# A hybrid decoder trunk on one core: TensorE's order where attention, output projection, norms and MLP meet

## The chip, the core and the metric

The kernel runs on one core of a Trainium2 chip. The core has a matrix engine (TensorE, PE in the profile's rows), whose weight loads are listed apart (PEld), a vector engine (VectorE, DVE), a scalar engine (ScalarE, ACT), GpSimd (POOL) and SyncE (SP), which only issues transfers here. Each engine works through its own list of instructions in order; semaphores make it wait for the others. The metric is the device time of one execution in microseconds (us).

## What is computed

A decoder trunk of two layers on 256 tokens of width 1024, in float32. Cut to what matters here, a layer is

```
h = rms_norm(x, ln1_gain[l]);  proj = h @ w_in[l]            # 1024 -> 2866 columns
o_nsa, o_mla, o_ret = three attention groups on slices of proj
x = x + concatenate([o_nsa, o_mla, o_ret]) @ w_out[l]         # 1024 -> 1024
h = rms_norm(x, ln2_gain[l])
x = x + square(relu(h @ w_up[l])) @ w_down[l]                 # 1024 -> 4096 -> 1024
```

and a last rms_norm follows the second layer. The change lies at the two places of a layer where x is normalised: between `w_out` and `w_up`, and between `w_down` and the next layer's `w_in`.

## The kernel before

**Tiles.** The 256 tokens are two tiles of 128 partitions, t = 0 and 1. `xs` holds the residual x of both tiles. Nearly every operand of a matmul is split into two parts, `hi` (a cast by ScalarE, line 140) and `lo` (the rest, a subtraction by VectorE, line 141); `mm3` (lines 146 to 148) makes a product of three matmuls, lo·hi, hi·lo and hi·hi. The up projection (`up_half`, lines 1023 and 1024) needs two instructions per product, a wide one of 512 columns and a narrow one of 256.

**Weights.** They come in units through one stream `W`: a load by SyncE into one of five raw buffers, then a split into one of five hi and lo buffers. A unit is split up to four units ahead of its use, unless `W.hold(key)` stops the splitting ahead of unit `key`; `W.release(after, n)` lets it go on, with the new splits issued behind the two instructions `after`. A unit's raw buffer takes the next load once its split is done.

**Norms.** The factor of a row is applied behind the projection, so ahead of it only the gain is needed. `norm_half(t, h, gain, eng)` takes half h (512 columns) of tile t: a product `xg` of xs and the gain (line 504), four transposes of 128x128 into a bank `ps_xT` (line 506), and the split of that bank into the two parts of `xT`, by ScalarE and VectorE. `sum_sq` is ScalarE's sum of squares (`junk`, line 512).

**The order.** Each engine's list is fixed before the run: a scheduler simulates the engines and takes at each point the ready instruction of highest priority (`prio`, from a table), and `tc.issue_after(x)` makes it place what stands inside behind x.

**From attention to MLP.** The second token tile's work comes last in some places and first in others: `TORD = (1, 0)`, so tile 1 goes first here. I call it the first tile, and tile 0 the second. The values of the selected and sliding attention (`nsa_values`) transpose probabilities into `ps_pT`, copy them to `pT` (`g == 0` by ScalarE, line 868, the other by VectorE, line 870), multiply them with the values into `l_oT`, and split that into `mixT`. The output projection runs over eight slices `kt` of mixT in the order 3, 4, 6, 7, 5, 0, 1, 2; only the last three need `nsa_values`. Its four banks `l_po` are two for the first tile (numbers 1823 and 1824 for halves 0 and 1 in the orders below) and two for the second (1821 and 1822). Then, at lines 999 to 1004, for the first tile and then the second, half by half, VectorE adds `l_po` to xs (line 1002) and `norm_half` is called, with GpSimd for the first tile's products and VectorE for the second's. Splits were held ahead of the unit `(l, "wu", 1, 0)` and are released behind the last of the four splits of xT; the four sums of squares come behind it too.

**MLP.** The up projection has 16 chunks c of 256 columns, each in two halves i of its depth. The first two chunks start together, half 0 of both and then half 1 of both (lines 1055 to 1057), into four banks `ps_up`. For each chunk ScalarE copies a part of `ps_up` to `u_s` and VectorE adds the rest (lines 1034 and 1035), which frees the bank; chunk 2 takes the banks of chunk 0. The down projection gathers in four banks `l_pd`.

**To the next layer.** For tile 0 and then tile 1, half by half, VectorE adds `l_pd` to xs and `norm_half` follows; the splits held ahead of the fourth A unit are released behind it, and so are the squares. The first projection of the next layer is chunk A (`inproj`, 434 columns, four weight units of two k slices each); within a unit it runs tile 0 and then tile 1. ScalarE evacuates the result to `l_a` (line 570, scaled by `l_rstd`), and TensorE transposes it (`ps_cT`, line 599).

Of the kernel before, what the change touches and what calls it, by code (L numbers as in the profile page):

```python
# [77 lines left out]
def tile_hybrid_trunk(  # L78
# [65 lines left out]
    def mm3(o, a, b, start, stop):  # L144

        nc.tensor.matmul(o, a[1], b[0], start=start, stop=False)  # L146
        nc.tensor.matmul(o, a[0], b[1], start=False, stop=False)  # L147
        nc.tensor.matmul(o, a[0], b[0], start=False, stop=stop)  # L148
# [338 lines left out]
    def norm_half(t, h, gain, eng=nc.vector):  # L487
        sl = slice(h * 512, (h + 1) * 512)
        xg = scr("xg", [P, 512])
        ps = wk("ps_xT", "MN"[h])  # L490
# [14 lines left out]
        for j in range(4):  # L505
            nc.tensor.transpose(ps[:, j * P:(j + 1) * P], xg[:, j * P:(j + 1) * P], ident)
        dst = (slice(None), slice(4 * h, 4 * h + 4), slice(t * P, (t + 1) * P))
        return split(xT[0][dst], xT[1][dst], ps.rearrange("p (k c) -> p k c", k=4))

# [18 lines left out]
    for l in range(DEPTH):  # L528
# [17 lines left out]
        for t in range(2):  # L546
            mean_sq(ms1, ss1, t)
            rsqrt(rstd[:, t:t + 1], ms1[:, t:t + 1])
            nc.gpsimd.tensor_scalar(hrstd[:, t:t + 1], rstd[:, t:t + 1], 0.5, None, op0=ALU.mult)

        if l == 0:
            rope_tables()
        mixT = [p1.tile([P, 8, S], F32R, name=f"{L}mixT{i}", tag=f"mixT{i}") for i in range(2)]

        def inproj(name, evac):
            n = CHUNKS[name][1]
            ps = [acc(f"{L}{name}{t}") for t in range(2)]
            for i, ks in enumerate(KSETS[n]):
                w = W.get((l, name, i))
                for t in range(2):  # L560
                    tk = slice(t * P, (t + 1) * P)
                    for j, kt in enumerate(ks):
                        mm3(ps[t][:, 0:n], (xT[0][:, kt, tk], xT[1][:, kt, tk]),
                            [z[:, j * n:(j + 1) * n] for z in w], start=kt == 0, stop=kt == 7)
# [275 lines left out]
        def nsa_values(t, prs):  # L840
# [38 lines left out]
            for r in range(3):  # L879
                nc.tensor.matmul(oT[:, r * P:(r + 1) * P], vcb[:, r].rearrange("p g d -> p (g d)"), pcT,  # L880
                                 start=False, stop=r == 2)
            split_mix(mixT, 0, 3, t, oT[:, 0:384].rearrange("p (k c) -> p k c", k=3))

        Pcs = [None, None]
# [102 lines left out]
        def outproj(kts, t):  # L987
            for h in range(2):
                for kt in kts:
                    w = W.get((l, "wo", kt))  # L990
                    mm3(po[t][h], [m[:, kt, t * P:(t + 1) * P] for m in mixT],
                        [z[:, h * 512:(h + 1) * 512] for z in w], start=kt == KORDER[0], stop=kt == KORDER[-1])

        W.hold((l, "wu", 1, 0))
        for kts in ((3,), (4,), (6,), (7,), (5,), (0, 1, 2)):
            for t in TORD:
                with prio("po" if len(kts) == 1 else "pol"):
                    outproj(kts, t)
        for t in TORD:
            for h in range(2):  # L1000
                sl = slice(h * 512, (h + 1) * 512)
                nc.vector.tensor_tensor(xs[:, t, sl], xs[:, t, sl], po[t][h], op=ALU.add)
                with prio("norm"):
                    last = norm_half(t, h, gains[f"b{l}"], nc.gpsimd if t == TORD[0] else nc.vector)
        W.release(last, SPLIT_AHEAD)
        with tc.issue_after(last[0].ins):
            for t in TORD:
                for h in range(2):
                    sum_sq(t, h, ss2)
                mean_sq(ms2, ss2, t)  # L1010
                nc.vector.reciprocal(rs2[:, t:t + 1], ms2[:, t:t + 1])


        pd = [[(att(f"{L}pd{t}{h}", "MN"[h]) if t else acc(f"{L}pd{t}{h}")) for h in range(2)] for t in range(2)]
        def up_half(c, i, ps):
# [3 lines left out]
            for k in range(4):  # L1019
                x2 = xT2[:, 4 * i + k].rearrange("p z c -> p (z c)")  # L1020
                for j in range(2):
                    o = k * 256 + j * P
                    nc.tensor.matmul(ps[j], w[0][:, o:o + P], x2, start=i == 0 and k == 0, stop=False)  # L1023
# [153 lines left out]
```

## Time and profile before

| | us |
|---|---|
| median of 3 runs | 675.86 (675.41 to 676.44) |
| profiled execution | 675.34 |
| its span, first to last instruction | 673.5 |
| TensorE busy in the span | 651.4 |
| VectorE busy | 452.4 |
| ScalarE busy | 379.3 |

The granted clock of TensorE was 0.993 of full speed on average over the span. TensorE is busy for 97% of it. The rows that the prediction reads stand further below: a row of a timeline gives the start, the duration, the engine, line, operation, its result and sources, and in square brackets how long the engine had been idle and whose signal ended that.

### The profile page before, as it was taken

Reading aid. Unit: us, or ns where it says so; the run is one execution under the profiler, and the core shown is the slowest. Engines: PE = TensorE matmul, PEld = TensorE weight load, DVE = VectorE, ACT = ScalarE, POOL = GpSimd, SP = SyncE. Lnnn points to the kernel's source line nnn. Section 1 sums busy time; section 2 is a strip of 40 time slices with the busy share of each in tenths; the row PEclk is TensorE's granted clock in tenths of the full one; section 3 lists DMA queues with packets and bytes.
Section 4 is the critical chain, followed back from the end, with each engine's and each line's share of the span. In section 5 each row is a group of like instructions: output and inputs, shape, how many; then the busy total and the mean of one; then the engine's idle time right before and its main releaser. Section 6 shows DMA issues by size and latency. Waiting matters only on the chain.

```text
span 673.5 us, 10414 instructions
## 1 busy us (share of the span) xinstructions
PE 651.4 (97%) x3639; PEld 551.9 (82%) x3639; DVE 452.4 (67%) x1051; ACT 379.3 (56%) x887; POOL 68.0 (10%) x116
## 2 busy tenths in 40 slices
PE   7988999999999999999999999999999999999995
PEld 6987978676788888888889998876688888888884
DVE  6755967677756666666685597677686666666664
ACT  5857776364645454545466786637284454545442
POOL 3510401201000000000023132111100000000000
PEclk7999999999999999999999999999999999999999
DMA  7898544122865656565648574331275656565511
GB/s 232 261 186 257 168 126 123 44 94 68 269 204 165 218 169 215 167 215 167 175 139 200 168 240 133 93 95 34 92 254 181 220 169 208 172 203 181 195 62 62
DMA packets 79508, 111.58 MB, mean 166 GB/s; under 512 B 9432, under 2 KB 67680, under 8 KB 79328
## 3 DMA queue, kind: packets, MB, share of 16 engines
q1 hardware_dynamic: 79424, 110.92, 53.9%
q8 instruction: 28, 0.46, 0.3%
q14 instruction: 24, 0.20, 0.1%
q0 software_dynamic: 32, 0.00, 0.0%
HBM read 109.86 MB, written 1.05 MB: 165 GB/s over the span
## 4 chain that ended last, share of the span: by engine, by line
PE 87%; DMA 5%; DVE 4%; ACT 1%; issue 1%; SPq 1%; POOL 0%; POOLq 0%; ACTq 0%; DVEq 0%
PE ps_up L1023 17%; PE l_pd L146 9%; PE l_pd L147 9%; PE l_pd L148 8%; PE ps_up L1024 8%; PE l_po L146 2%; PE l_po L148 2%; PE l_po L147 2%; PE l_oT L856 2%; DMA raw_B<-in_w_in_dram 2%; PE l_B L146 1%; PE l_B L147 1%; PE l_B L148 1%; PE ps_pT L864 1%; PE ps_s L146 1%; DMA raw_wu<-in_w_up_dram 1%
## 5 line engine op out<-in xcount | busy, mean ns | idle before, releaser
L1023 PE MATMUL ps_up<-xT,hi_wu 128*128 128x512 f32 x512 | 180.0, 394 | 1.3 <-DVE u_s L1035 1.3
L1024 PE MATMUL ps_up<-xT,lo_wu 128*128 128x256 f32 x512 | 140.7, 279 | 0.0
L1023 PEld LDWEIGHTS ps_up<-xT,hi_wu 128*128 128x128 f32 x512 | 95.7, 187 | 24.0 <-DVE u_s L1035 1.7
L141 DVE TENSOR_TENSOR lo_wd<-raw_wd,hi_wd 128x1024 fp32r<-128x1024 f32 x64 | 78.2, 1225 | 52.5 <-ACT hi_wd L140 52.2
L147 PE MATMUL l_pd<-lo_wd,u_h 128*128 128x512 f32 x256 | 100.1, 391 | 0.0
L146 PE MATMUL l_pd<-hi_wd,u_l 128*128 128x512 f32 x256 | 100.1, 391 | 0.0
L148 PE MATMUL l_pd<-hi_wd,u_h 128*128 128x512 f32 x256 | 99.6, 389 | 0.0
L1024 PEld LDWEIGHTS ps_up<-xT,lo_wu 128*128 128x128 f32 x512 | 96.0, 188 | 1.7
L140 ACT CAST hi_wu<-raw_wu 128x512 fp32r<-128x512 f32 x128 | 72.5, 617 | 38.9 <-issue 28.1
L141 DVE TENSOR_TENSOR lo_wu<-raw_wu,hi_wu 128x512 fp32r<-128x512 f32 x128 | 82.2, 687 | 16.6 <-ACT hi_wu L140 16.4
L140 ACT CAST hi_wd<-raw_wd 128x1024 fp32r<-128x1024 f32 x64 | 67.0, 1049 | 32.1 <-PE l_pd L148 21.4
L146 PEld LDWEIGHTS l_pd<-hi_wd,u_l 128*128 128x128 f32 x256 | 48.0, 188 | 10.8
L148 PEld LDWEIGHTS l_pd<-hi_wd,u_h 128*128 128x128 f32 x256 | 48.1, 188 | 10.4
L147 PEld LDWEIGHTS l_pd<-lo_wd,u_h 128*128 128x128 f32 x256 | 48.1, 188 | 8.9
L140 ACT CAST u_h<-u_u 128x512 fp32r<-128x512 f32 x32 | 19.8, 620 | 55.4 <-DVE u_u L1037 55.4
L141 DVE TENSOR_TENSOR lo_B<-raw_B,hi_B 128x192 fp32r<-128x192 f32 (+1 forms) x80 | 28.7, 415 | 23.9 <-ACT hi_B L140 23.8
L1034 ACT COPY u_s<-ps_up 128x256 f32<-128x256 f32 x64 | 23.3, 368 | 36.1 <-PE ps_up L1024 36.1
L1035 DVE TENSOR_TENSOR u_s<-ps_up,u_s 128x256 f32<-128x256 f32 x64 | 26.7, 421 | 24.8 <-ACT u_s L1034 24.8
L140 ACT CAST hi_B<-raw_B 128x192 fp32r<-128x192 f32 (+1 forms) x80 | 25.1, 381 | 18.6 <-DMA raw_B<-in_w_in_dram 13.7
L146 PE MATMUL l_B<-hi_B,xT 128*128 128x384 f32 x96 | 32.9, 351 | 2.3 <-ACT q_sb L570 2.3
L141 DVE TENSOR_TENSOR u_l<-u_u,u_h 128x512 fp32r<-128x512 f32 x32 | 22.1, 691 | 17.8 <-ACT u_h L140 17.8
L148 PE MATMUL l_B<-hi_B,xT 128*128 128x384 f32 x96 | 32.4, 338 | 0.0
(321 smaller groups left out, 1246.5 us busy)
## 6 DMA issues: line engine op xcount, KB each, us to landing
raw_wu<-in_w_up_dram SPq DMA_DIRECT2D x64, 512.0 KB, 4.6
raw_wd<-in_w_down_dram SPq DMA_DIRECT2D x64, 512.0 KB, 4.2
raw_B<-in_w_in_dram SPq DMA_DIRECT2D x24, 384.0 KB, 3.6
raw_wo<-in_w_out_dram SPq DMA_DIRECT2D x10, 512.0 KB, 3.6
raw_A<-in_w_in_dram SPq DMA_DIRECT2D x8, 434.0 KB, 5.0
raw_wo<-in_w_out_dram SPq DMA_DIRECT2D x12, 256.0 KB, 3.8
raw_w<-in_cmp_w_k_dram SPq DMA_DIRECT2D x8, 256.0 KB, 6.3
raw_w<-in_cmp_w_v_dram SPq DMA_DIRECT2D x8, 256.0 KB, 5.8
```

What stands on the lines that cost most here:

```text
L140: a = nc.scalar.copy(out=hi, in_=src)
L141: b = eng.tensor_tensor(lo, src, hi.bitcast(F32), op=ALU.subtract)
L146: nc.tensor.matmul(o, a[1], b[0], start=start, stop=False)
L147: nc.tensor.matmul(o, a[0], b[1], start=False, stop=False)
L148: nc.tensor.matmul(o, a[0], b[0], start=False, stop=stop)
L856: nc.tensor.matmul(oT[gp, 0:384], kv_sb[kt][:, vi, gp], pTs[g][:, 0:384], start=i == 0, stop=False)
L864: last = nc.tensor.transpose(ps[:, r * P:(r + 1) * P], prs[g][:, r, o:o + P], ident)
L1023: nc.tensor.matmul(ps[j], w[0][:, o:o + P], x2, start=i == 0 and k == 0, stop=False)
L1024: nc.tensor.matmul(ps[j][:, 0:S], w[1][:, o:o + P], x2[:, 0:S], start=False, stop=i == 1 and k == 3)
L1034: nc.scalar.copy(sj, ps[j][:, S:512])
L1035: nc.vector.tensor_tensor(sj, ps[j][:, 0:S], sj, op=ALU.add)
```

## The change

It alters no number that is computed and no weight that is loaded; it alters the order of instructions and the banks of some of them.

*Output projection and norms.* The last three slices of mixT are taken half by half: first tile, half 0; then its half 1, placed behind the last instruction of `nsa_values` of the second tile; then both halves of the second tile behind the transposes of the first. `add_norm` is the addition, the product and `norm_half` of one half; its transposes get an explicit place (`behind`) and, but for half 0 of the second tile, a bank of the pools that were used for `l_po` and `l_oT` and not those of `wk`. Half 0 of the first tile is transposed behind its half 1's products, and so on. The last of the four, half 1 of the second tile, is transposed behind `up_half(0, 0)`, inside the MLP. `W.hold` stops one unit later, ahead of `(l, "wu", 0, 1)`, so that chunk 1's half 0 is split before the release. The first up matmul is placed behind the first tile's last transposes.

*To the next layer.* Chunk A is done by tile: two units of tile 0, then the transposes, the release and the squares of tile 1 (`second_norm`), and the rest. `factors` holds the row factors, which stood ahead of the projection.

```diff
     def mm3(o, a, b, start, stop):
...
+        return nc.tensor.matmul(o, a[0], b[0], start=False, stop=stop)
...
-    def norm_half(t, h, gain, eng=nc.vector):
+    def norm_half(t, h, gain, eng=nc.vector, ps=None, behind=None):
...
-        ps = wk("ps_xT", "MN"[h])
+        if ps is None:
+            ps = wk("ps_xT", "MN"[h])
...
+        with tc.issue_after(behind.ins) if behind else nullcontext():
+            for j in range(4):
+                last_tr[0] = nc.tensor.transpose(ps[:, j * P:(j + 1) * P], xg[:, j * P:(j + 1) * P], ident)
...
         def inproj(name, evac):
...
+            steps = [(i, t) for i in range(len(KSETS[n])) for t in range(2)]
+            if name == "A" and l:
+                steps.sort(key=lambda z: z[1])
+            for at, (i, t) in enumerate(steps):
+                if name == "A" and l and at == 2:
+                    second_norm(last)
+                    factors()
...
-        W.hold((l, "wu", 1, 0))
-        for kts in ((3,), (4,), (6,), (7,), (5,), (0, 1, 2)):
+        W.hold((l, "wu", 0, 1))
+        for kt in (3, 4, 6, 7, 5):
             for t in TORD:
...
+        first, second = TORD
+        def add_norm(t, h, behind=None):
+            sl = slice(h * 512, (h + 1) * 512)
+            nc.vector.tensor_tensor(xs[:, t, sl], xs[:, t, sl], po[t][h], op=ALU.add)
+            ps = acc("ps_xT") if t == first else att("ps_xT", "N") if h else None
+            with prio("norm"):
+                return norm_half(t, h, gains[f"b{l}"], nc.gpsimd if t == first else nc.vector, ps, behind)
+        with prio("pol"):
+            outproj((0, 1, 2), first, (0,))
+            last_po = outproj((0, 1, 2), first, (1,), nsa_end[second])
+        add_norm(first, 0, last_po)
+        with prio("pol"):
+            outproj((0, 1, 2), second, (0,), last_tr[0])
+            last_po = outproj((0, 1), second, (1,), last_tr[0])
+        add_norm(second, 0, last_po)
+        with prio("pol"):
+            last_po = outproj((2,), second, (1,), last_tr[0])
+        add_norm(first, 1, last_po)
+        tr_first = last_tr[0]
...
-        for i in range(2):
-            for c in range(2):
-                up_half(c, i, pu[c])
+        last = up_half(0, 0, pu[0], tr_first)
+        last = add_norm(second, 1, last)
+        W.release(last, SPLIT_AHEAD)
...
+        up_half(1, 0, pu[1])
+        for c in range(2):
+            up_half(c, 1, pu[c])
...
+                if t == 0:
+                    with prio("norm"):
+                        norm_half(t, h, gains[f"a{l + 1}"], nc.gpsimd, behind=pd_last[1][h])
+        def second_norm(behind, l=l, ss_next=ss_next):
+            for h in range(2):
                 with prio("norm"):
-                    last = norm_half(t, h, gains[f"a{l + 1}"], nc.gpsimd if t == 0 else nc.vector)
-        W.release(last, SPLIT_AHEAD)
...
+                    last = norm_half(1, h, gains[f"a{l + 1}"], nc.vector, behind=behind)
+            W.release(last, SPLIT_AHEAD)
```

TensorE's list in layer 0, from the end of the output projection into the MLP, in the kernel before (`hi_wu_0_1915` is half 0 of chunk 0's up weights, `hi_wu_0_2015` half 0 of chunk 1, `hi_wu_1_2021` half 1 of chunk 0):

```order
L146 MATMUL l_po_1822<-hi_wo_1895,l_mixT_197 128x512
L147 MATMUL l_po_1822<-lo_wo_1896,l_mixT_196 128x512
L148 MATMUL l_po_1822<-hi_wo_1895,l_mixT_196 128x512
L506 MATMUL ps_xT<-c0s,xg 128x128 x8
L1023 MATMUL ps_up<-xT,hi_wu_0_1915 128x512
L1024 MATMUL ps_up<-xT,lo_wu_0_1916 128x256
```

The same list in the changed kernel, where `hi_wu_0_1935` is half 0 of chunk 1 and `hi_wu_1_2047` and `hi_wu_1_2053` are half 1 of chunks 0 and 1:

```order
L508 MATMUL ps_xT<-c0s,xg 128x128 x4
L1052 MATMUL ps_up<-xT,lo_wu_0_1936 128x256
L1051 MATMUL ps_up<-xT,hi_wu_0_1935 128x512
L1052 MATMUL ps_up<-xT,lo_wu_0_1936 128x256
L1051 MATMUL ps_up<-xT,hi_wu_1_2047 128x512 x2
L1051 MATMUL ps_up<-xT,hi_wu_1_2053 128x512 x2
```

All transposes stood ahead of the first up matmul; now four of them stand behind 29 up matmuls of half 0 (16 of chunk 0, 13 of chunk 1), three up matmuls ahead of the first one of half 1.

In the kernel before, the last mixT and xT casts on ScalarE and what follows them, down to the copy that frees the first up bank (`hi_wd`: down weights, `hi_wu_0_2117`: half 0 of chunk 2):

```order
L140 CAST xT<-ps_xT 128x4x128 x4
L140 CAST hi_wu_0_2015<-raw_wu_0_1661 128x512
L140 CAST hi_wu_1_2021<-raw_wu_1_1687 128x512
L140 CAST hi_wu_1_2027<-raw_wu_1_1825 128x512
L140 CAST hi_wu_0_2015<-raw_wu_0_1661 128x512
L140 CAST hi_wu_1_2021<-raw_wu_1_1687 128x512
L140 CAST hi_wu_1_2027<-raw_wu_1_1825 128x512
L140 CAST hi_wd_0_2073<-raw_wd_0_1853 128x1024
L512 ACTIVATE junk,l_ss_1818<-xs 128x512 x4
L140 CAST hi_wd_1_2095<-raw_wd_1_1873 128x1024
L140 CAST hi_wu_0_2117<-raw_wu_0_1893 128x512 x2
L1034 COPY u_s<-ps_up 128x256
```

The changed kernel's ScalarE, from the casts of chunk 1's half 0 on:

```order
L140 CAST hi_wu_0_1935<-raw_wu_0_1661 128x512 x2
L881 COPY pT<-ps_pT 128x384
L891 COPY pcT<-ps_pcT 96x128
L140 CAST l_mixT_196<-l_oT_1317 128x3x128
L140 CAST xT<-ps_xT 128x4x128 x4
L140 CAST hi_wu_1_2047<-raw_wu_1_1687 128x512
L140 CAST hi_wu_1_2053<-raw_wu_1_1825 128x512
L140 CAST hi_wd_0_2059<-raw_wd_0_1853 128x1024
L140 CAST hi_wu_1_2047<-raw_wu_1_1687 128x512
L140 CAST hi_wu_1_2053<-raw_wu_1_1825 128x512
L140 CAST hi_wd_1_2095<-raw_wd_1_1873 128x1024
L140 CAST hi_wu_0_2117<-raw_wu_0_1893 128x512 x2
```

Two half casts of chunk 1's half 0 went from behind the four xT casts to ahead of the pT copy; the four squares follow the last row here, and then the first `u_s` copies. Further up in TensorE's list six output-projection matmuls of the first tile (of slice 2) went from ahead of the last three `ps_pT` transposes to behind the value products (of the half-1 matmuls nine in all stand there now), and the raw buffer that the extra split frees lets SyncE issue the load of chunk 2's half 0 ahead of the next gain.

TensorE's list from layer 0's last down matmul to chunk A of layer 1, before:

```order
L148 MATMUL l_pd_2048<-hi_wd_1_3494,u_h 128x512
L506 MATMUL ps_xT<-c0s,xg 128x128 x16
L146 MATMUL l_A_3694<-hi_A_3527,xT 128x434
L147 MATMUL l_A_3694<-lo_A_3528,xT 128x434
L148 MATMUL l_A_3694<-hi_A_3527,xT 128x434
```

and after:

```order
L148 MATMUL l_pd_2014<-hi_wd_1_3494,u_h 128x512
L508 MATMUL ps_xT<-c0s,xg 128x128 x8
L146 MATMUL l_A_3646<-hi_A_3527,xT 128x434
L147 MATMUL l_A_3646<-lo_A_3528,xT 128x434
L148 MATMUL l_A_3646<-hi_A_3527,xT 128x434
```

Eight of the sixteen transposes, those of tile 1, left this place; they stand behind the twelfth l_A matmul now. VectorE's list here reads the same in both kernels: the addition and the product of both halves of tile 1 stand ahead of the four lo parts of xT.

## Rows read from the trace of the kernel before

**Rows 1.** Busy time, share of the span and instructions of each engine.

```profile
PE 651.4 (97%) x3639; PEld 551.9 (82%) x3639; DVE 452.4 (67%) x1051; ACT 379.3 (56%) x887; POOL 68.0 (10%) x116
```

**Rows 2.** Timeline (start, duration in us) of TensorE, output projection to MLP, layer 0.

```profile
149.75 0.82 PE L864 MATMUL ps_pT<-c0s,p_nsa 128*128 128x128 f32 x6
...
154.90 1.04 PE L506 MATMUL ps_xT<-c0s,xg 128*128 128x128 f32 x8
156.22 0.50 PE L146 MATMUL l_po<-hi_wo,l_mixT 128*128 128x512 f32 x1 [0.29 <-DVE l_mixT L141]
...
160.52 0.60 PE L506 MATMUL ps_xT<-c0s,xg 128*128 128x128 f32 x4
162.19 0.66 PE L506 MATMUL ps_xT<-c0s,xg 128*128 128x128 f32 x4 [1.07 <-DVE xg L504]
162.79 0.51 PE L1023 MATMUL ps_up<-xT,hi_wu 128*128 128x512 f32 x1
...
175.66 0.49 PE L1023 MATMUL ps_up<-xT,hi_wu 128*128 128x512 f32 x1 [1.35 <-DVE u_s L1035]
```

**Rows 3.** Timeline of ScalarE in the same stretch.

```profile
147.74 1.14 ACT L140 CAST hi_wu<-raw_wu 128x512 fp32r<-128x512 f32 x2
...
150.44 0.48 ACT L868 COPY pT<-ps_pT 128x384 f32<-128x384 f32 x1 [1.56 <-PE ps_pT L864]
...
161.16 0.59 ACT L140 CAST xT<-ps_xT 128x512 fp32r<-128x512 f32 x1 [4.54 <-PE ps_xT L506]
162.88 0.59 ACT L140 CAST xT<-ps_xT 128x512 fp32r<-128x512 f32 x1 [1.14 <-PE ps_xT L506]
163.36 3.23 ACT L140 CAST hi_wu<-raw_wu 128x512 fp32r<-128x512 f32 x6
166.49 1.05 ACT L140 CAST hi_wd<-raw_wd 128x1024 fp32r<-128x1024 f32 x1
...
169.90 1.04 ACT L140 CAST hi_wd<-raw_wd 128x1024 fp32r<-128x1024 f32 x1
```

**Rows 4.** Timeline of VectorE in the same stretch.

```profile
150.61 0.56 DVE L870 COPY pT<-ps_pT 128x384 f32<-128x384 f32 x1 [0.76 <-PE ps_pT L864]
...
158.62 0.69 DVE L1002 TENSOR_TENSOR xs<-xs,l_po 128x512 f32<-128x512 f32 x1 [1.18 <-PE l_po L148]
...
163.50 0.69 DVE L141 TENSOR_TENSOR xT<-ps_xT,xT 128x512 fp32r<-128x512 f32 x1 [0.76 <-ACT xT L140]
```

**Rows 5.** Busy time by engine, layer 1's first two up chunks; columns: PE, PEld, DVE, ACT, POOL.

```profile
488.88:500.14 11.26, 11.26 (x65) 9.81 (x65) 9.07 (x17) 10.67 (x23) 0.00 (x0) 1.00 0.68 241
```

**Rows 6.** Timelines of TensorE, VectorE and ScalarE at layer 1's chunk A.

```profile
343.92 0.63 PE L506 MATMUL ps_xT<-c0s,xg 128*128 128x128 f32 x4 [0.57 <-DVE xg L504]
344.42 0.46 PE L146 MATMUL l_A<-hi_A,xT 128*128 128x434 f32 x1
...
354.06 0.49 PE L599 MATMUL ps_cT<-c0s,l_a 128*128 128x128 f32 x3
...
343.69 2.48 DVE L141 TENSOR_TENSOR xT<-ps_xT,xT 128x512 fp32r<-128x512 f32 x4
...
344.58 0.59 ACT L140 CAST xT<-ps_xT 128x512 fp32r<-128x512 f32 x1 [0.51 <-PE ps_xT L506]
...
350.93 0.93 ACT L140 CAST hi_B<-raw_B 128x384 fp32r<-128x384 f32 x2 [0.41 <-PE l_A L148]
352.12 0.93 ACT L140 CAST hi_B<-raw_B 128x384 fp32r<-128x384 f32 x2 [0.26 <-ACT hi_B L140]
353.13 0.62 ACT L570 ACTIVATE l_a<-l_A,l_rstd 128x434 f32<-128x434 f32 x1
```

**Rows 7.** Costliest groups: busy us, mean ns of one, idle before; up chunks' evacuation.

```profile
L1034 ACT COPY u_s<-ps_up 128x256 f32<-128x256 f32 x64 | 23.3, 368 | 36.1 <-PE ps_up L1024 36.1
L1035 DVE TENSOR_TENSOR u_s<-ps_up,u_s 128x256 f32<-128x256 f32 x64 | 26.7, 421 | 24.8 <-ACT u_s L1034 24.8
```

**Rows 8.** The chain of waits that ended last: a load in layer 0.

```profile
166.62 6.60 DMA raw_wu<-in_w_up_dram
```

**Rows 9.** DMA issues of layer 1's burst: KB, median us from issue to landing.

```profile
raw_wd<-in_w_down_dram SPq DMA_DIRECT2D x1, 512.0 KB, 5.4
```

More of the change, by code (lines that the diff above doesn't have):

```diff
@@ L545, in tile_hybrid_trunk, with factors @@
             ss1 = ss_next
[L546 to L549, printed above, removed]
+        def factors():
+            for t in range(2):
+                mean_sq(ms1, ss1, t)
+                rsqrt(rstd[:, t:t + 1], ms1[:, t:t + 1])
+                nc.gpsimd.tensor_scalar(hrstd[:, t:t + 1], rstd[:, t:t + 1], 0.5, None, op0=ALU.mult)
         if l == 0:
+            factors()
             rope_tables()
@@ L985, in tile_hybrid_trunk, with outproj @@
         po = [[(acc(f"{L}po{t}{h}") if t == TORD[0] else (wk(f"{L}po{t}{h}", "M") if h else att(f"{L}po{t}{h}", "M"))) for h in range(2)] for t in range(2)]
-        def outproj(kts, t):
-            for h in range(2):
+        def outproj(kts, t, hs=(0, 1), behind=None):
+            last = None
+            for h in hs:
                 for kt in kts:
                     w = W.get((l, "wo", kt))
-                    mm3(po[t][h], [m[:, kt, t * P:(t + 1) * P] for m in mixT],
-                        [z[:, h * 512:(h + 1) * 512] for z in w], start=kt == KORDER[0], stop=kt == KORDER[-1])
@@ L994, in tile_hybrid_trunk @@
-        W.hold((l, "wu", 1, 0))
-        for kts in ((3,), (4,), (6,), (7,), (5,), (0, 1, 2)):
-            for t in TORD:
[L997 to L1004, printed above, removed]
@@ L1005, in tile_hybrid_trunk @@
-        W.release(last, SPLIT_AHEAD)
[L1006 to L1011, printed above, removed]
+                    with tc.issue_after(behind.ins) if behind else nullcontext():
+                        last = mm3(po[t][h], [m[:, kt, t * P:(t + 1) * P] for m in mixT],
+                                   [z[:, h * 512:(h + 1) * 512] for z in w], start=kt == KORDER[0],
+                                   stop=kt == KORDER[-1])
@@ L1022, in up_half @@
                     o = k * 256 + j * P
-                    nc.tensor.matmul(ps[j], w[0][:, o:o + P], x2, start=i == 0 and k == 0, stop=False)
-                    nc.tensor.matmul(ps[j][:, 0:S], w[1][:, o:o + P], x2[:, 0:S], start=False, stop=i == 1 and k == 3)
+                    with tc.issue_after(behind.ins) if behind else nullcontext():
+                        nc.tensor.matmul(ps[j], w[0][:, o:o + P], x2, start=i == 0 and k == 0, stop=False)
+                    last = nc.tensor.matmul(ps[j][:, 0:S], w[1][:, o:o + P], x2[:, 0:S], start=False,
+                                            stop=i == 1 and k == 3)
+            return last
         def up_act(ps):
@@ L1045, in down @@
                     for j in range(2):
-                        mm3(pd[t][h], [z[:, j * S + t * P:j * S + (t + 1) * P] for z in us],
-                            [z[:, h * 512:(h + 1) * 512] for z in w[j]],
-                            start=c == 0 and j == 0, stop=c == NU - 1 and j == 1)
+                        last = mm3(pd[t][h], [z[:, j * S + t * P:j * S + (t + 1) * P] for z in us],
+                                   [z[:, h * 512:(h + 1) * 512] for z in w[j]],
+                                   start=c == 0 and j == 0, stop=c == NU - 1 and j == 1)
+                    pd_last[t][h] = last
         def up_banks(c):
```

43 lines of the change are left out of this document (25 added, 18 removed).

## The prediction, before the result was known

> **What bounds the kernel now.** I read the share of busy time first: TensorE is busy for 651.4 of 673.5 us [rows 1], so whatever a new order gains or loses must be time in which TensorE stands still, or starts late and never catches up. Next I read its timeline where the change works, which is three places: the step from the output projection to the MLP in layer 0 (150 to 176 us), the same step in layer 1, and the step from layer 0's MLP to layer 1's input projection (341 to 354 us). TensorE waits there for 0.29 us (mixT), 1.07 us (the last xg) and 1.35 us (a bank of the next up chunk, layer 0 only) [rows 2], and for 0.57 us at the input projection [rows 6]. Layer 1's step repeats the first two waits 326.09 us later, without the third: its 64 up matmuls run 11.26 us without a gap [rows 5]. All that a better order could take away is thus 2 x (0.29 + 1.07) + 1.35 + 0.57 = 4.64 us. Last I read ScalarE and VectorE in the same windows [rows 3, 4, 6], because each works through its own list in order: ScalarE stood idle for 4.54 us before an xT cast, although the weight casts that it ran next, from 163.36 on, were free of that cast [rows 3]. That row decides the forecast.
>
> From [rows 5], a pair of up matmuls (hi, lo) takes 11.26 / 32 = 0.352 us; an output-projection matmul 0.233 us (18 between 156.22 and 160.52, less 0.1 for the first after a wait); four transposes 0.4 to 0.6 us [rows 2].
>
> **The change at the output projection, up to the first up matmul (layer 0's clock).** Six matmuls (1.40 us) that stood before six transposes of probabilities now stand after the value products, and nothing ahead of them moves, so those transposes start at 148.35 instead of 149.75 [rows 2], and only three matmuls (to 149.63) lie between them and the last three transposes. These need the bank that ScalarE's pT copy frees. ScalarE now splits one more weight unit before that copy: two casts, 1.04 us by their spacing, behind the pair that started at 147.74, so the copy runs from 149.85 to 150.33 instead of starting at 150.44 [rows 3]. TensorE waits 0.75 us. VectorE is free at 149.85 [rows 4] and now has a copy (0.56), two lo parts of the new unit and one xs addition (0.61 to 0.69 each, as the like-sized operations in [rows 4]) before the second copy, which ends at about 152.75; the value product waits 0.95 us. TensorE then ends the value products at 154.0. The nine matmuls put behind them (2.1 us) cover the way of mixT (154.90 to 156.22, 1.32 us, in [rows 2]): this wait of 0.29 us is gone. Four transposes and fifteen matmuls follow, to 160.0. The next transposes need xg of the second tile, whose addition and product take VectorE 0.69 + 0.69 us after the ninth of these matmuls ends [rows 4]; six matmuls (1.40 us) cover 1.65 us not quite: 0.25 us of waiting. After four transposes, three matmuls and four transposes, up waits for the lo part of xT, which is there 2.0 us after its transposes began (162.19 to 164.19 [rows 2, 4]): 0.43 us. The first up matmul starts at 162.3 instead of 162.79, but four transposes are still owed. So this stretch gains nothing: two old waits (1.36 us) give way to four new ones.
>
> **The same step, from the first up matmul on.** The last four transposes stand after 29 up matmuls (14.5 pairs, 5.16 us), so they start at 167.48. Their xg is ready at about 164.3, but nothing can be issued past what stands before it. ScalarE's cast of them starts 0.69 us later (162.19 to 162.88 [rows 2, 3]), at 168.17, and until then ScalarE can do none of the casts that stand behind: it idles some 5 us. Behind it, before it frees the bank of the next up chunk, lie: the xT cast itself 0.48 us, six half casts of up weights 3.13 us, a down cast and four squares 3.41 us, a second down cast 0.95 us (1.04 of duration less the overlap with its neighbour) [rows 3], 7.97 us in all, then the u_s copy (0.37), VectorE's addition (0.42) [rows 7] and the signals. The next up chunk's first matmul can start at 177.0. TensorE has only four transposes and 17.5 pairs (6.2 us) left, so it waits about 1.1 us for the lo part of the late xT and 1.9 us for the bank. Before, the same chain hung on transposes at 162.19 and had all 32 pairs as cover.
>
> In layer 1 the chunk began at 500.14, that is 174.05 on layer 0's clock [rows 5]: **loss 2.95 us**. In layer 0 it began at 175.66 after the wait of 1.35 us [rows 2], which came from an up load issued at 166.62 and landed 6.60 us later [rows 8]. That load is now issued at about 152 us, since the extra early split frees its buffer, and this wait goes; the new chain ends later still: **loss 1.35 us**. The following load now waits for a split at 172.6 instead of 167.2. It must land by about 177.1, 4.5 us later; [rows 8, 9] show 6.6 and 5.4 us for loads in such a burst. I take no cost (its matmuls stand 1.4 us behind the chunk's first), with 0 to 1.3 us per layer as the bounds. Everything after is TensorE's own back-to-back work, so losses stay to the end.
>
> **The change at layer 1's input projection.** Tile 0's eight transposes, twelve matmuls of tile 0, tile 1's eight transposes, then the rest. VectorE's list is the same as before: both xs and xg of tile 1 still stand ahead of the four lo parts of xT, which start at 343.69 [rows 6]. So the first matmul still starts at 344.42, and what TensorE used to do in its wait, tile 1's transposes, is now owed: eight of them, 0.9 us. A matmul takes 0.20 us here (48 of them between 344.42 and 354.06 [rows 6]), so they start at 344.42 + 12 x 0.20 = 346.8 and end at 347.85. ScalarE's last xT cast moves from 344.58 to 348.3 (3.7 us), and with it all that stands behind: the A3 and uq weights, four squares, uk, four halves of B2 weights, and the evacuation of A, whose result TensorE transposes next. ScalarE had 0.41 + 0.26 us of idle time in that list [rows 6], so the evacuation starts 2.7 to 3.0 us later than 353.13 and the transposes at 354.06 start at 356.5. **Loss 2.4 us**, of which 0.9 is owed work, 0.3 a wait for the lo part of tile 1 and 1.2 to 1.4 the wait for ScalarE. Below, 0.9 us (if ScalarE's list had more slack than I see); above, 3.6 us, as the B weight loads wait for splits that come 3.3 to 3.7 us later while their users come 2.4 later.
>
> **Sum.** 1.35 + 2.95 + 2.4 = 6.7 us on the profiled execution's 675.34 us (span 673.5): 682.0 us. The median of the runs is 675.86, so I say 682.5.
>
> **The rivals.** *Faster: the order covers its waits.* The transposes have banks of their own and matmuls ahead of them; if the late casts cost TensorE nothing, all 4.64 us go: 675.86 - 4.64 = 671.2 us. It needs the next chunk's bank free within the 6.6 us of work behind the late transposes; [rows 3] give 9.5 us. The Trainium skill (Perfetto Trace Analysis, Matmuls) advises rotating independent groups through different banks so that one's evacuation overlaps the next one's matmuls; by that advice this change would help, but the row in which ScalarE idles before the cast shows a wait of another kind. Chance 0.08.
> *No difference.* The MLP steps come out even, layer 0's wait of 1.6 us (174.05 to 175.66) goes and only the input projection costs 2.4: 676.7 us. It needs ScalarE's list to be some 3 us shorter than [rows 3] make it. Chance 0.07.
> *Slower still: the loads are late.* Both layers pay the upper bound of the burst: 682.5 + 1.3 to 2.6 = 683.8 to 685.1 us. For it speaks the 6.6 us landing, against it the 5.4 [rows 8, 9]. Chance 0.15.
>
> **How the numbers follow.** The forecast has 0.70, the rivals 0.08, 0.07 and 0.15. Measurement tells 0.2% (1.35 us) from no change. Faster 0.08, within 0.2% 0.07, slower 0.85. The range leaves out the first two and a little of each end: the forecast with 0.9 at the input projection and 0.7 of each MLP loss is 679.7; with some room for a shorter list 678.0; above, late loads in both layers and 3.6 at the input projection give 686.0.
>
> **What would show it.** Right: in layer 1, the first up matmul at about 162.3 + 326.1 plus the earlier delay, an idle time of about 1 us before the first hi_wu of the second half (released by VectorE's xT), one of about 2 us before the next chunk (released by VectorE's u_s), ScalarE idle some 5 us before the last xT cast; at the input projection 1.7 us before l_A and over 1 us before ps_cT, released by ScalarE. Wrong: if ScalarE ran weight casts during that idle time, if ps_cT follows l_A without a gap, or if the waits are there and a later one of the profile before is gone in exchange.

## Result

The changed kernel takes 682.62 us (median of 4 runs, 681.68 to 684.27) against 675.63 us before (4 runs, 673.23 to 676.44): a ratio of 1.0107, 95% interval 1.0084 to 1.0130. It is slower by 7.0 us. The profiled execution took 681.68 us with a span of 679.9 us at a granted clock of 0.993, the same clock as before. One of the five executions of early_release below took 1623.96 us; its ratio leaves that one out.

The span grew by 6.4 us (673.5 to 679.9). TensorE's busy time, for the same number of instructions, grew by 2.3 of them [rows 1], its idle time by 4.1 (22.1 to 26.2); the other engines' busy times differ by less than 2 us:

```profile
PE 653.7 (96%) x3639; PEld 551.0 (81%) x3639; DVE 452.2 (67%) x1051; ACT 378.5 (56%) x887; POOL 69.8 (10%) x116
```

The profile counts an instruction as busy up to its own end, and in a dense row that lies behind the next one's start (0.39 us long, one every 0.23 below); so the first part of a wait still counts as busy time.

TensorE's timeline of the changed kernel, output projection to MLP in layer 0, answering [rows 2]:

```profile
147.64 0.82 PE L877 MATMUL ps_pT<-c0s,p_nsa 128*128 128x128 f32 x6
...
148.76 0.39 PE L148 MATMUL l_po<-hi_wo,l_mixT 128*128 128x512 f32 x1
149.62 0.55 PE L877 MATMUL ps_pT<-c0s,p_nsa 128*128 128x128 f32 x3 [0.48 <-ACT pT L881]
150.10 0.87 PE L869 MATMUL l_oT<-pT,l_kv 128*64 128x384 f32 x4
...
151.14 1.63 PE L869 MATMUL l_oT<-pT,l_kv 128*64 128x384 f32 x4
...
153.39 0.48 PE L146 MATMUL l_po<-hi_wo,l_mixT 128*128 128x512 f32 x1
153.72 0.39 PE L147 MATMUL l_po<-lo_wo,l_mixT 128*128 128x512 f32 x1
153.95 0.39 PE L148 MATMUL l_po<-hi_wo,l_mixT 128*128 128x512 f32 x1
...
155.58 0.60 PE L508 MATMUL ps_xT<-c0s,xg 128*128 128x128 f32 x4
155.94 0.48 PE L146 MATMUL l_po<-hi_wo,l_mixT 128*128 128x512 f32 x1
156.25 0.39 PE L147 MATMUL l_po<-lo_wo,l_mixT 128*128 128x512 f32 x1
...
159.27 0.40 PE L148 MATMUL l_po<-hi_wo,l_mixT 128*128 128x512 f32 x1
159.78 0.66 PE L508 MATMUL ps_xT<-c0s,xg 128*128 128x128 f32 x4
...
160.97 0.60 PE L508 MATMUL ps_xT<-c0s,xg 128*128 128x128 f32 x4
161.84 0.50 PE L1051 MATMUL ps_up<-xT,hi_wu 128*128 128x512 f32 x1 [0.27 <-DVE xT L141]
...
167.09 0.60 PE L508 MATMUL ps_xT<-c0s,xg 128*128 128x128 f32 x4
...
169.18 1.18 PE L1051 MATMUL ps_up<-xT,hi_wu 128*128 128x512 f32 x4 [1.02 <-DVE xT L141]
...
176.55 0.50 PE L1051 MATMUL ps_up<-xT,hi_wu 128*128 128x512 f32 x1 [1.50 <-DVE u_s L1065]
```

The two old waits, 0.29 us for mixT and 1.07 us for xg, are gone. In their place stand 0.48 us for ScalarE's pT copy, 0.76 us inside the second group of value products (1.63 us for four, where the first four took 0.87), 0.28 us ahead of the transposes at 159.78 (the matmul before them started at 159.27, and these matmuls come every 0.23 us) and 0.27 us for xT. Then come the two that cost: 1.02 us for the late xT and 1.50 us for the bank of the next chunk. ScalarE's timeline there, answering [rows 3], shows whose work they wait for:

```profile
149.10 0.47 ACT L881 COPY pT<-ps_pT 128x384 f32<-128x384 f32 x1
...
161.60 0.59 ACT L140 CAST xT<-ps_xT 128x512 fp32r<-128x512 f32 x1 [0.55 <-PE ps_xT L508]
167.72 0.58 ACT L140 CAST xT<-ps_xT 128x512 fp32r<-128x512 f32 x1 [5.53 <-PE ps_xT L508]
168.20 1.14 ACT L140 CAST hi_wu<-raw_wu 128x512 fp32r<-128x512 f32 x2
...
173.22 0.63 ACT L516 ACTIVATE junk<-xs 128x512 f32<-128x512 f32 x1
...
175.69 0.62 ACT L1064 COPY u_s<-ps_up 128x256 f32<-128x256 f32 x2
```

It stands idle for 5.53 us ahead of the late cast, and then works through 7.97 us without a pause (167.72 to 175.69) before it starts the copy that frees a bank, together with VectorE's addition. Layer 1 repeats this 329.9 us later, with the same two waits of 1.02 and 1.50 us.

Layer 1's input projection, TensorE and then ScalarE, answering [rows 6]:

```profile
342.78 1.03 PE L508 MATMUL ps_xT<-c0s,xg 128*128 128x128 f32 x8
345.33 0.47 PE L146 MATMUL l_A<-hi_A,xT 128*128 128x434 f32 x1 [1.51 <-DVE xT L141]
...
347.83 1.04 PE L508 MATMUL ps_xT<-c0s,xg 128*128 128x128 f32 x8
...
357.34 0.55 PE L612 MATMUL ps_cT<-c0s,l_a 128*128 128x128 f32 x3 [0.94 <-ACT l_a L583]
...
348.80 1.07 ACT L140 CAST xT<-ps_xT 128x512 fp32r<-128x512 f32 x2 [4.31 <-PE ps_xT L508]
...
356.67 0.62 ACT L583 ACTIVATE l_a<-l_A,l_rstd 128x434 f32<-128x434 f32 x1
```

From its first xT transposes to ps_cT this place takes 14.56 us; before it took 12.19 (341.87 to 354.06).

### The profile page after: what moved, and what is told of

Same layout as the page of the kernel before. It is cut to its first block, busy times and chain, and to the rows that moved or that the text cites. A ratio compares the mean times of both kernels' runs of the same rounds, so it can differ in the third digit from the quotient of the medians.

```text
span 679.9 us, 10412 instructions
## 1 busy us (share of the span) xinstructions
PE 653.7 (96%) x3639; PEld 551.0 (81%) x3639; DVE 452.2 (67%) x1051; ACT 378.5 (56%) x887; POOL 69.8 (10%) x116
## 4 chain that ended last, share of the span: by engine, by line
PE 85%; ACT 4%; DMA 4%; DVE 3%; issue 2%; SPq 1%; POOL 0%; POOLq 0%; ACTq 0%
PE ps_up L1051 17%; PE l_pd L146 8%; PE l_pd L147 8%; PE l_pd L148 8%; PE ps_up L1052 8%; PE l_po L146 2%; PE l_oT L869 2%; PE l_po L148 2%; PE l_po L147 2%; DMA raw_B<-in_w_in_dram 1%; PE l_B L148 1%; PE l_B L146 1%; PE l_B L147 1%; ACT hi_wu L140 1%; PE ps_pT L877 1%
## 5 line engine op out<-in xcount | busy, mean ns | idle before, releaser
L141 DVE TENSOR_TENSOR u_l<-u_u,u_h 128x512 fp32r<-128x512 f32 x32 | 22.1, 691 | 17.9 <-ACT u_h L140 17.9
```

The source lines that it names most:

```text
L141: b = eng.tensor_tensor(lo, src, hi.bitcast(F32), op=ALU.subtract)
```

## Where the 7 us are

Runs differ by some microseconds in layer 0 ahead of the changed places, so I compare stretches of the traces between fixed points. They repeat to a few hundredths of a microsecond where order and granted clock are the same, but for layer 0 in the order of before (see below the table). "Layer 0" and "layer 1" run from the first matmul of the projection l_rq to the first matmul of the third up chunk; "MLP step" is the part of layer 1 from the first up matmul on; "input projection" is that from the first xT transposes to ps_cT.

| kernel | median, us | layer 0 | layer 1 | MLP step | input projection |
|---|---|---|---|---|---|
| before | 675.63 | 108.57 | 107.10 | 11.37 | 12.19 |
| after | 682.62 | 110.19 | 110.20 | 14.71 | 14.56 |
| mlp_only | 679.86 | 111.74 | 110.22 | 14.73 | 12.20 |
| bound_only | 676.96 | 107.71 | 107.08 | 11.35 | 14.55 |
| a_ahead | 681.44 | 111.73 | 110.20 | 14.73 | 12.21 |
| transposes_ahead | 679.53 | 108.29 | 108.29 | 12.81 | 14.56 |
| part_release | 679.67 | 108.46 | 108.44 | 12.96 | 14.56 |
| early_release (stretches: an execution of 681.56 us) | 684.08 | 111.03 | 109.48 | 13.99 | 14.56 |
| squares_late | 685.92 | 112.85 | 111.50 | 16.02 | 14.57 |
| best_d | 671.36 | 106.01 | 106.03 | 11.75 | 12.21 |

After less before: 1.62 + 3.10 + 2.37 = 7.1 us, the measured 7.0. (The spans of the two profiles differ by only 6.4, because l_rq began 0.73 us earlier in the second one.) The 1.62 us of layer 0 depend on the execution of the kernel before: bound_only has the same order there and took 107.71 us, not 108.57, since ScalarE waited less for the load of chunk 2's up weights. The rows of before, then of bound_only:

```profile
173.32 1.14 ACT L140 CAST hi_wu<-raw_wu 128x512 fp32r<-128x512 f32 x2 [2.38 <-DMA raw_wu<-in_w_up_dram]
...
172.40 1.15 ACT L140 CAST hi_wu<-raw_wu 128x512 fp32r<-128x512 f32 x2 [1.53 <-DMA raw_wu<-in_w_up_dram]
...
174.73 0.51 PE L1042 MATMUL ps_up<-xT,hi_wu 128*128 128x512 f32 x1 [0.48 <-DVE u_s L1056]
```

TensorE's wait for the bank was 1.35 us in the one and 0.48 in the other. Against bound_only the change costs layer 0 2.5 us. Layer 1, where the kernel before has no such wait, is the surer measure.

The medians come from four sets of runs. The kernel before had 675.63 us in the set of the changed kernel, 676.02 in that of mlp_only, bound_only, transposes_ahead and early_release, 674.96 in that of part_release, squares_late and best_d, and 674.89 in that of a_ahead. So medians of different sets compare to about 1 us only; the ratios below are against the kernel before.

In the layer 0 column, mlp_only, a_ahead and squares_late hold another 1.5 us that has nothing to do with the edits; the last section shows it.

## The experiments

**Which part costs what.** *mlp_only* keeps the new step to the MLP and takes the layer boundary back; *bound_only* does the reverse.

```diff
-            if name == "A" and l:
-                steps.sort(key=lambda z: z[1])
...
-                    second_norm(last)
...
+                    last = norm_half(t, h, gains[f"a{l + 1}"], nc.gpsimd if t == 0 else nc.vector)
+        W.release(last, SPLIT_AHEAD)
```

> The step from output projection to MLP as changed, layer 1's input projection as before. Theory (ScalarE's list behind the late transposes costs 1.6 us in layer 0 and 3.0 to 3.4 us in layer 1): 675.6 + 4.6 to 5.0 = 680.4 us, with waits of 1.0 us for the late xT and of 1.5 us for u_s in both layers, as in the changed kernel. Rival (the loss sits at the input projection, the MLP steps come out even): 675.6 us.

Measured: 679.86 us, ratio 1.0080 (1.0052 to 1.0107). TensorE waits 1.03 us for the late xT and 1.51 us for u_s in both layers, as in the changed kernel, and the input projection is back at 12.20 us.

```diff
-        W.hold((l, "wu", 0, 1))
+        W.hold((l, "wu", 1, 0))
...
-        last = up_half(0, 0, pu[0], tr_first)
-        last = add_norm(second, 1, last)
...
+        for i in range(2):
+            for c in range(2):
+                up_half(c, i, pu[c])
```

> Layer 1's input projection as changed, the two steps to the MLP as before. Theory: 675.6 + 2.4 = 678.0 us; l_A starts after a wait of about 1.5 us, ScalarE's last xT cast comes about 3.7 us later than before, and ps_cT waits about 1 us for l_a. Rival (a part's cost depends on the other part, for instance through the loads): nearer to 675.6 or above 679.

Measured: 676.96 us, ratio 1.0021 (0.9998 to 1.0044). By the ratios the two excesses are 5.4 and 1.4 us, 6.8 together, where the whole change has 7.2; but each has an interval of about 1.7 us to either side, and by the medians of their own set they are only 3.8 and 0.9. So the times alone do not show that the parts add up, nor settle bound_only's 2.4 us. The traces do: bound_only has l_A behind a wait of 1.51 us, ps_cT behind one of 0.97 us and 14.55 us for the stretch, and in each of the two kernels the part that is kept takes what it takes in the changed kernel, and the other what it took before (layer 1 and input projection in the table). The parts don't depend on each other.

**What costs at the input projection.** *a_ahead* keeps the order of the matmuls by tile, and puts tile 1's transposes ahead of all of them.

```diff
-                if name == "A" and l and at == 2:
-                    second_norm(last)
+                if name == "A" and l and at == 0:
+                    second_norm(None)
```

> The changed kernel, but at layer 1's input projection tile 1's eight transposes, release and squares stand ahead of the first l_A matmul again; the order of the matmuls by tile stays. Theory (the 2.4 us there come from the eight transposes behind twelve matmuls, by the work that is owed and by ScalarE's list behind the last xT casts): l_A waits 0.6 us for xg at the transposes as before, the last xT cast comes within 1 us of the first matmul, ps_cT follows without a wait, 682.6 - 2.4 = 680.2 us. Rival (the order by tile costs, since it wants all four A units in the time of two and holds their buffers longer): 682 us or more, with a wait inside l_A or ahead of ps_cT.

Measured: 681.44 us, ratio 1.0087 (1.0053 to 1.0120); the stretch is back at 12.21 us, with the old wait of 0.57 us for xg and none ahead of ps_cT. The order by tile costs nothing; the place of the eight transposes, with the release and the squares that moved with them, costs all of the 2.37 us. How the 2.37 divide into owed work and waits is read from the rows and was not tested by itself. The median fell by only 1.2, and the interval holds the rival's 682 as well as 680.2: the stretch decides here, not the time.

**What costs at the step to the MLP: the place of the late transposes.** *transposes_ahead* takes the constraint away that put them behind chunk 0's half 0; the scheduler then puts chunk 1's half 0 first and the transposes behind its 16 matmuls, not behind 29; chunk 0's half 0 follows them.

```diff
-        last = up_half(0, 0, pu[0], tr_first)
-        last = add_norm(second, 1, last)
+        last = add_norm(second, 1, tr_first)
         W.release(last, SPLIT_AHEAD)
+        up_half(0, 0, pu[0], last_tr[0])
```

> The changed kernel with the late four transposes behind 16 up matmuls (chunk 1's half 0 goes first) instead of 29; release and squares still behind their cast. Theory: they start 2.44 us earlier, the 1.0 us wait for the late xT goes, and ScalarE's list behind the cast, 9.46 us from the transposes to the next chunk in the changed kernel, ends 2.44 us earlier too: 682.6 - 2 x 2.44 = 677.7 us, with a u_s wait of about 0.5 us left. Rival (the place does not matter, the squares and the casts behind the release are late for another reason, such as loads): 682 us.

Measured: 679.53 us, ratio 1.0056 (1.0035 to 1.0078). The wait for the late xT is gone and the one for u_s is 0.85 us. The step is 1.9 us shorter per layer, not 2.44. The first u_s copy does start 2.33 us sooner (11.52 us behind the first up matmul, not 13.85), but here the split of chunk 2 came behind the squares, so VectorE's two lo parts (174.29 to 175.50) stand right ahead of its u_s addition:

```profile
174.29 1.29 DVE L141 TENSOR_TENSOR lo_wu<-raw_wu,hi_wu 128x512 fp32r<-128x512 f32 x2
175.50 0.42 DVE L1065 TENSOR_TENSOR u_s<-ps_up,u_s 128x256 f32<-128x256 f32 x1
```

That addition starts 0.81 us behind the copy at 174.69; in the changed kernel it is 0.40 us (175.69 to 176.09). These 0.41 us account for the difference between 2.33 and 1.9.

**Or ScalarE's idle time?** *part_release* leaves the late transposes where the change put them, and lets ScalarE split the two held up units behind the third xT cast.

```diff
+        def release_to(self, after, key):
...
+            self.limit = self.index[key]
+            with tc.issue_after(after[0].ins), tc.issue_after(after[1].ins):
+                self.split_to(min(self.limit, self.loaded))
...
-        add_norm(first, 1, last_po)
+        W.release_to(add_norm(first, 1, last_po), (l, "wd", 0, 0))
```

> The changed kernel, but the two held up units (half 1 of chunks 0 and 1) are split behind the first tile's last xT cast; everything from the down weights on stays behind the late cast. Theory (ScalarE's idle time ahead of the late cast is the loss): four casts, 2.1 us, move into the idle 5.5 us, VectorE's four lo parts, 2.4 us, end before the late xT comes, the first u_s copy starts some 2.1 us earlier than in the changed kernel, the 1.5 us waits go and the 1.0 us waits stay: 682.6 - 3.0 = 679.6 us. Rival (the late place costs by itself): 682 us or more.

Measured: 679.67 us, ratio 1.0062 (1.0040 to 1.0084). That this is the expected time to 0.1 us is luck: the two steps together gave back 3.5 us, not 3.0, and in its trace layer 1's l_rq waits 1.42 us for l_kv, where the changed kernel's waits 0.62. Its ScalarE, and TensorE's remaining wait:

```profile
162.02 2.18 ACT L140 CAST hi_wu<-raw_wu 128x512 fp32r<-128x512 f32 x4
167.66 0.59 ACT L140 CAST xT<-ps_xT 128x512 fp32r<-128x512 f32 x1 [3.45 <-PE ps_xT L514]
...
173.54 0.35 ACT L1070 COPY u_s<-ps_up 128x256 f32<-128x256 f32 x1
...
169.02 0.50 PE L1057 MATMUL ps_up<-xT,hi_wu 128*128 128x512 f32 x1 [0.94 <-DVE xT L141]
```

The late cast comes as late as before (5.89 us after the first up matmul; 5.88 in the changed kernel), four casts have moved into the idle time, the u_s copy starts 2.1 us sooner, and no wait for u_s is left. So ScalarE's held list was 1.75 us of the loss in each layer (14.71 to 12.96); the wait for the late xT (0.94 us here) belongs to the place of the transposes.

**The same with more released.** *early_release* moves the whole release there, down weights included.

```diff
-        add_norm(first, 1, last_po)
+        W.release(add_norm(first, 1, last_po), SPLIT_AHEAD)
...
         last = add_norm(second, 1, last)
-        W.release(last, SPLIT_AHEAD)
```

> The changed kernel, but the held splits are released behind the first tile's last xT cast instead of behind the late one; the late transposes stay where they are. Theory (the loss is ScalarE standing idle 5.5 us with weight casts that it could have done): ScalarE runs six casts, 4.0 us, in that idle time, the bank is free in time, the 1.5 us waits for u_s go in both layers and the 1.0 us waits for the late xT stay: 682.6 - 3.0 = 679.6 us. Rival (the late place of the transposes costs by itself, whatever ScalarE does): 682 us or more.

Measured: 684.08 us, ratio 1.0123 (1.0077 to 1.0170): a miss. The rows below are from an execution of 681.56 us.

> A second look at the kernel whose splits are released behind the first tile's last xT cast, since its times (684.1 us) fell on the rival's side and its profile is of an execution with a TensorE that ran at less than half its pace from end to end. Theory: ScalarE filled its idle time, but with down-weight casts too, one of which waits for a buffer, and VectorE's list got six lo parts ahead of the lo part of the late xT, so the 1.0 us wait for the late xT grows to 2 us or more while the 1.5 us u_s wait shrinks. Rival (the late transposes cost by themselves): both waits stand as in the changed kernel.

ScalarE and TensorE in layer 0:

```profile
164.22 1.14 ACT L140 CAST hi_wu<-raw_wu 128x512 fp32r<-128x512 f32 x2
167.31 1.05 ACT L140 CAST hi_wd<-raw_wd 128x1024 fp32r<-128x1024 f32 x1 [1.95 <-PE ps_up L1051]
168.26 0.58 ACT L140 CAST xT<-ps_xT 128x512 fp32r<-128x512 f32 x1
...
170.28 0.50 PE L1051 MATMUL ps_up<-xT,hi_wu 128*128 128x512 f32 x1 [1.98 <-DVE xT L141]
```

The down cast ahead of the late xT cast waits for a buffer that TensorE still reads, and VectorE's 1.23 us for its lo part stands ahead of the lo part of xT. The wait for u_s is gone, that for xT has grown from 1.02 to 1.98 us. Layer 1 gains 0.72 us (14.71 to 13.99) where I had expected 1.5, and layer 0 even loses, for a reason that the last section shows. The second theory stands: the wait that was put into ScalarE's list was passed on to TensorE.

**A shorter list.** *squares_late* puts the four squares, 2.46 us, behind the first u_s copies.

```diff
-        with tc.issue_after(last[0].ins):
-            for t in TORD:
-                for h in range(2):
-                    sum_sq(t, h, ss2)
...
         us = [up_act(z) for z in pu]
+        with tc.issue_after(u_last[0].ins):
+            for t in TORD:
+                for h in range(2):
+                    sum_sq(t, h, ss2)
```

> The changed kernel with ScalarE's four sums of squares, 2.46 us, placed behind the first u_s copies, nothing else moved by hand. Theory: between the late xT cast and the first u_s copy lie 6.5 us instead of 7.97 (one more split moves ahead of the copy), so the u_s wait of 1.5 us shrinks to about 0.1 in both layers: 682.6 - 2.8 = 679.8 us. Rival (a later load or split takes the place of the squares): 682 us, with the wait still about 1.5 us.

Measured: 685.92 us, ratio 1.0146 (1.0114 to 1.0178): a miss, on the rival's side. ScalarE and TensorE in layer 0:

```profile
174.58 1.15 ACT L140 CAST hi_wu<-raw_wu 128x512 fp32r<-128x512 f32 x2
177.84 1.14 ACT L140 CAST hi_wu<-raw_wu 128x512 fp32r<-128x512 f32 x2 [2.11 <-DMA raw_wu<-in_w_up_dram]
178.88 0.64 ACT L1066 COPY u_s<-ps_up 128x256 f32<-128x256 f32 x2
...
180.17 0.50 PE L1051 MATMUL ps_up<-xT,hi_wu 128*128 128x512 f32 x1 [2.72 <-DVE u_s L1067]
```

With the squares gone the scheduler put a split ahead of the copy whose load had not landed: 2.11 us of waiting for a DMA, in the list ahead of u_s (2.19 us in layer 1). In the changed kernel this split stands behind the copies. So taking out 2.46 us of squares, which waited for nothing, made room for a cast that had to wait. A version with the squares late and this split still behind the copies was not run, so what the squares cost by themselves is open. The profiled execution, 689.53 us, is the slowest of the five.

**A version from these.** *best_d* takes the new order at the output projection, and nothing at the layer boundary; the hold of before (no extra split ahead of the pT copy); the release in two steps of part_release; the late transposes behind 16 up matmuls; and the squares behind u_s.

```diff
-        W.hold((l, "wu", 0, 1))
+        W.hold((l, "wu", 1, 0))
...
+        W.release_to(add_norm(first, 1, last_po), (l, "wd", 0, 0))
...
-        up_half(1, 0, pu[1])
+        up_half(1, 0, pu[1], last_tr[0])
```

> What the theory says should beat both: the changed order at the output projection, but the splits held as before the change, the three held up units split behind the first tile's last xT cast, the late transposes behind 16 up matmuls (chunk 0's half 0) and ahead of chunk 1, the squares behind the first u_s copies; the layer boundary as before the change. Waits left per layer: 0.25 us (xg) and 0.27 us (xT) against 1.36 us before, and layer 0's 1.35 us for u_s gone: 675.6 - 1.7 - 1.35 = 672.6 us. Rival (new waits for the lo parts, which VectorE makes in a row, take what is gained): 675.6 us or more.

Measured: 671.36 us (6 runs, 670.50 to 673.05), ratio 0.9938 (0.9915 to 0.9960): faster than both. It takes several steps at once, so its time shows that the new order can pay, and not what each step is worth. TensorE and ScalarE:

```profile
161.03 0.50 PE L1051 MATMUL ps_up<-xT,hi_wu 128*128 128x512 f32 x1 [0.27 <-DVE xT L141]
...
163.94 0.60 PE L514 MATMUL ps_xT<-c0s,xg 128*128 128x128 f32 x4
...
161.28 3.22 ACT L140 CAST hi_wu<-raw_wu 128x512 fp32r<-128x512 f32 x6
164.57 0.59 ACT L140 CAST xT<-ps_xT 128x512 fp32r<-128x512 f32 x1
...
169.07 1.14 ACT L140 CAST hi_wu<-raw_wu 128x512 fp32r<-128x512 f32 x2 [2.02 <-DMA raw_wu<-in_w_up_dram]
```

Six casts fill ScalarE's time up to the late xT, which is cast 0.63 us behind the start of its transposes, as in the changed kernel (167.09 to 167.72). The wait for the load is there too (2.02 us), but earlier, and the u_s copies behind it are still in time. From l_rq to the first up matmul layer 1 takes 94.28 us, against 95.49 in the changed kernel: with the hold of before, the waits of 0.48 and 0.76 us around the pT copies are gone, which shows that the extra early split made them. Against the kernel before, layer 1 gains 1.07 us: 1.45 up to the first up matmul, less 0.38 in the MLP step, where the four transposes are still owed. Layer 0 gains 2.56 us, since its wait for the bank (1.35 us in that trace of before) is gone too.

## Why the prediction was right

It said 682.5 us (678.0 to 686.0) and slower; the time is 682.62. It was right in each of its main steps, on the reason that an engine "works through its own list in order".

| step | predicted | measured |
|---|---|---|
| pT copy, value product, xg, first up: new waits | 0.75, 0.95, 0.25, 0.43 | 0.48, 0.76, 0.28, 0.27 |
| first up matmul, against before | 0.49 earlier | 0.22 earlier |
| ScalarE idle ahead of the late cast | some 5 | 5.53 |
| waits for the late xT and for the bank | 1.1 and 1.9 | 1.02 and 1.50 |
| first up matmul to the third chunk | 14.7 | 14.71 |
| layer 0 and layer 1 | 1.35 and 2.95 | 1.62 and 3.10 |
| waits ahead of l_A and ps_cT | 1.7 and over 1 | 1.51 and 0.94 |
| input projection | 2.4 | 2.37 |

("0.22 earlier": 161.84 against 162.79, less the 0.73 us by which the second profile was ahead at l_rq.) The terms that were off are small ones of the first stretch, which came out 0.27 us too early. With the measured times put on the clock of before, the last three pT transposes began at 150.35 (worked out: 150.38), the matmuls behind the value products at 154.12 (154.0), the second tile's transposes at 160.51 (160.25) and the first up matmul at 162.57 (162.3). So about 0.12 us had gathered by the end of the value products, and the rest by the second tile's transposes. The rows show where that rest comes from: the first matmul behind a group of small ones takes some 0.32 us to the next one (153.39 to 153.72, 155.94 to 156.25) and not 0.23, twice on this way.

The waits in the first line of the table look smaller than forecast mainly by the way of counting. The prediction counted from when the next instruction could have started; 0.48 and 0.27 are idle times behind the profile's end of the instruction before. Counted from start to start (0.23 us for a matmul, 0.36 for four transposes, by 155.58 to 155.94) they are 0.63 and 0.51, and the four waits come to 2.2 us against 2.38. One step of the sum was wrong without harm: with the second pT copy ending at 152.75, as it says, the value products behind it would end at about 154.4, by the 1.64 us that they take in the kernel before (153.26 to 154.90), and not at 154.0. In the changed kernel the wait came inside the group and cost 0.7 to 0.8 us, so that 154.0 was nearly met. That is luck.

The 0.27 us carried into both layers: in layer 1 the third chunk began at 500.25 before, 0.11 us later than the end of the window in [rows 5] that I took for it; with it I would have forecast 2.84 us, so that both layers are off by the same 0.27. Two agreements are luck as well. Layer 0's 1.35 us rest on one execution of the kernel before: against bound_only's layer 0 (107.71) the loss is 2.5. And that 682.5 and 682.62 lie 0.1 us apart means little, where the four runs lie between 681.68 and 684.27.

The point on which the forecast turned was the place of the late cast in ScalarE's list. part_release and transposes_ahead show both halves of it: letting ScalarE work in its idle time gives back 1.75 us per layer (14.71 to 12.96), a place 13 matmuls earlier 1.9 us. Both shorten the same chain, so the two don't add up.

None of the rivals came. The order did not cover its waits and the MLP steps did not come out even, since ScalarE's list of 7.97 us was as long as worked out. The early split did bring chunk 2's first load forward, to 151.42, and layer 0's old wait for it is gone. The load that follows was issued at 171.58, when its buffer came free, and landed 3.8 us later, more than 1 us ahead of the third chunk; so the late loads cost nothing in the changed kernel. In squares_late the same load did hold TensorE up, by way of ScalarE.

## What to carry to other kernels

When TensorE's order is changed to cover a wait, follow the engine that consumes the moved result: its list is in order too, so a result that comes late holds back everything that was listed behind it, even what does not need it, and the cost appears at the next bank that this engine frees. Before a wait is covered by a late step, move what is independent ahead of that step in the other engines' lists, and only as much as is sure to be ready: four casts that could run paid 1.75 us per layer, and the down casts that early_release adds, one of which had to wait for a buffer, took over half of it back in layer 1 (12.96 to 13.99). And look at what moves up when a list is shortened: in squares_late 2.46 us of squares made way for a cast that waited 2.11 us for its load, and the bank came free later than before.

## What the runs showed of the hardware

After a pause of about 2 us TensorE sometimes went on at its lower clock level. In a_ahead, layer 0, ahead of l_rq (a timeline row, and the busy times with the granted clock third from last):

```profile
67.96 0.41 PE L146 MATMUL l_rq<-hi_rq,xT 128*128 128x320 f32 x1 [2.13 <-ACT l_kv L583]
...
64.80:67.96 3.16, 1.03 (x6) 0.57 (x5) 2.06 (x6) 1.62 (x5) 0.00 (x0) 1.00 0.87 266
67.96:71.40 3.44, 3.44 (x14) 3.44 (x15) 3.10 (x12) 3.02 (x10) 2.25 (x9) 0.55 0.75 244
```

The granted clock was 0.55 over the 3.4 us behind the pause, that is mostly 1.2 GHz in place of 2.4, and the way from l_rq to l_rk took 10.78 us where the kernel before took 9.24 (67.09 to 76.33) at a clock of 1.00: a cost of 1.5 us. mlp_only and squares_late show the same there, behind pauses of 1.77 and 2.09 us (granted clock 0.61 and 0.72 over the next 3.4 us); before, best_d and transposes_ahead show none of it, behind 2.03, 2.25 and 2.42 us (1.00). So the length of the pause alone does not tell. It hit early_release in layer 0, behind its wait of 1.98 us for the late xT:

```profile
170.00:172.00 2.00, 1.73 (x9) 1.53 (x10) 1.22 (x5) 2.00 (x6) 0.00 (x0) 0.91 0.99 369
172.00:174.00 2.00, 2.00 (x8) 1.71 (x8) 0.76 (x3) 0.34 (x2) 0.00 (x0) 0.50 0.84 270
```

which is why its layer 0 step took 15.56 us and layer 1's, behind 1.97 us at full clock, 13.99. In squares_late both pauses ahead of the third chunk (2.72 and 2.79 us) were followed by it (0.70 and 0.57 over the next 3.3 and 3.5 us). None of the 1.0 to 1.5 us waits of the changed kernel was. A wait that grows towards 2 us can thus cost 1.5 us more than itself. What this does to the scatter of the runs is open. Over 21 runs of the kernel before (672.97 to 679.25 us) the mean granted clock lay between 0.986 and 0.995; the two runs at 0.986 took 677.24 and 679.25 us, but one at 0.992 took 678.38, so the clock is not all of it.
